# Output and down projection of a two-layer hybrid backbone: 512-column blocks with the k loop outside

## The chip, the cores and the metric

The kernel runs on one core of a Trainium2 chip, in one launch, all in float32 (the large products in the float32r format). The metric is the device time in microseconds (us); the figure for the kernel before is the median of three runs.

## The reference, cut to what matters

640 tokens (128 context tokens and 512 latent tokens) pass through two layers. Each layer has a token mixer and a feed-forward part. Only the two products marked below are touched by the change.

```python
def layer(x, cond, s0_h, s0_r, pos, p):
    ...
    h = rmsnorm(x, p["norm_mix"]) * (1.0 + sc_m) + sh_m
    y, S_a, S_b = token_mixers(h, p, s0_h, s0_r, pos)   # ends in concat([o_a, o_b]) @ p["w_out"]   <- touched
    x = x + g_m * y
    h = rmsnorm(x, p["norm_ffn"]) * (1.0 + sc_f) + sh_f
    gate, up = jnp.split(h @ p["w_up"], 2, axis=-1)
    x = x + g_f * ((jax.nn.silu(gate) * up) @ p["w_down"])   # <- touched
```

`w_out` is 1024 x 1024 and `w_down` is 2816 x 1024, one of each per layer. After the last layer comes a final RMSNorm and the output of `x`.

## The kernel before, in words

The tokens are five tiles of 128 (`NT` = 5, index t), the model width 1024 is eight blocks of 128 (`KT` = 8), the feed-forward width 2816 is 22 blocks, taken in two chunks of 11 (`CH`). Every float32 product is made of three float32r matmuls: each operand is split into a high and a low part, and high·high, high·low and low·high are accumulated (the three `mm` lines of every matmul helper).

Weights come in slots of at most 1024 columns per partition. `Stream.load` issues the DMA of a slot into one of three `raw` buffers on SyncE's queue; `Stream.cut` makes the high part with ScalarE (`wh`, L75) and the low part with VectorE (`wl`, L76) into one of four buffers (`W_BUFS`). `take(n)` hands out the next n cut slots, and `done(n)` gives them back and pumps: it cuts and loads the next slots as far as buffers allow.

Two helpers do nearly all products. `ws` keeps the weights as the stationary operand and moves 320 token columns (256 and 384 where `mid` is set). `as_` keeps 128 tokens as the stationary operand and moves 256 weight columns: for each token tile it goes through all k blocks into one PSUM tile, calls `evac`, and goes to the next token tile. PSUM is a pool of four tiles of 1024 columns (`psp`, two banks each); everything in the kernel takes its PSUM from there.

The output projection `w_out` does four blocks of 256 columns. Blocks 0 and 1 go through `as_`. Blocks 2 and 3 go through `as2`, in the order of pairs (block, tile) that is written out by hand in `OUT_ORDER`, with the four slots of both blocks held. The down projection (in `ffn`) does four blocks of 256 columns for each of the two chunks of 11 k blocks, with three slots (4 + 4 + 3 k blocks) held for each block. `evac` calls `x_add`: VectorE multiplies the PSUM columns by the gate (L957) and adds them to `x` (L959), and ScalarE squares the new columns with a row sum (`sq`, L548). After the last columns of a token tile, `add_norm` forms the reciprocal root, scales the tile, and puts its transposes and modulation (`norm_b`, `norm_c`) into a list that is worked off later by a clock of the generators' own cost units (`LAG`). The next product, the `ws` of three units with `mid` set, begins with token tiles 0 and 1 and needs the others in its second half. After the last layer `final` takes the place of `add_norm`.

Beside the main stream run "lanes": the `ada` lane computes modulation vectors, two VectorE operations per 256 KB of `ada_w` (L504), stepped by the cost units that the main generators yield (`Q_ADA`). Its eight column chunks in the feed-forward part of layer 0 each end in eight transposes into a PSUM tile `pc` and a reduction (L517). At the start of the last block of layer 0 the rest of that lane is drained. The buffers of `ada_w` are the same two `ad` buffers that `x_add` uses.

The order on each engine comes from the framework: it takes the program order as priority and places an instruction when its model holds it ready and has a buffer for it. It also sets all semaphores and buffer releases. Only the start (`boot`) is in an order written by hand.

Of the kernel before, what the change touches and what calls it, by code (L numbers as in the profile page):

```python
# [14 lines left out]
ALU = mybir.AluOpType  # L15
AX = mybir.AxisListType

P = 128
DM = 1024
KT = DM // P  # L20
NT = 5
TOK = NT * P
HALF = TOK // 2
DEPTH = 2
# [18 lines left out]
KD = 2  # L43
FAST = (0, 1, 3)
CUT = 256
OUT_ORDER = [(2, 0), (3, 0), (2, 1), (3, 1), (2, 2), (2, 3), (2, 4), (3, 2), (3, 3), (3, 4)]
Q_SCAN = 2.65
Q_ADA = (3.0, 2.0, 4.0)
ADP_BUFS = 2
# [6 lines left out]
class Stream:  # L56
    def __init__(self, net, slots):
        self.net, self.slots = net, slots
        self.loaded = self.split = self.used = 0
        self.raw, self.ready = {}, {}  # L60
# [42 lines left out]
class Net:  # L103
# [848 lines left out]

    def x_add(self, gates, n0, t, ps, slot):
        nc = self.nc
        g = gates[0 if t == 0 else 1][:, n0:n0 + 256]
        tmp = self.adp.tile([P, 512], F32, tag="ad", name="xa")
        nc.vector.tensor_tensor(tmp[:, :256], ps, g, op=ALU.mult)  # L957
        xs = self.x[:, t, n0:n0 + 256]
        nc.vector.tensor_tensor(xs, xs, tmp[:, :256], op=ALU.add)  # L959
        if slot is not None:  # L960
            self.sq(t, n0, 256, slot, tmp[:, 256:])

    def w_out(self, l):
        self.finish("ada", (l, "gm"))

        def src(i, t):
            return self.oT[i][:, 0, t * P:(t + 1) * P], self.oT[i][:, 1, t * P:(t + 1) * P]
        for n in range(2):
            def evac(g, ps):
                t, = g  # L970
                self.flushT()
                self.x_add(self.g_m, 256 * n, t, ps[:, :256], n)
            yield from self.as_(src, 2, [[t] for t in range(NT)], evac)
        if l == 0:
            self.finish("ada", (0, "cf"))
        self.new_hT()

        def evac2(n, t, ps):
            self.x_add(self.g_m, 256 * n, t, ps[:, :256], n)
            if n == 3:  # L980
                self.add_norm(t, l, 1)
        yield from self.as2(src, OUT_ORDER, evac2)

    def as2(self, ksrc, order, evac):
        slots = self.W.take(4)
        mm = self.nc.tensor.matmul
        for n, t in order:
            ps = self.ps("ga")
            o = ps[:, :256]
            for i in range(KT):  # L990
                hi, lo = slots[2 * (n - 2) + i // 4]
                j = i % 4
                a_hi, a_lo = ksrc(i, t)
                mm(o, a_hi, hi[:, j], start=i == 0, stop=False)  # L994
                mm(o, a_hi, lo[:, j], start=False, stop=False)  # L995
                mm(o, a_lo, hi[:, j], start=False, stop=i == KT - 1)  # L996
                if i == 3:
                    yield 1.31
            if t == NT - 1:
                self.W.done(2, n == 2)  # L1000
            evac(n, t, ps)
            yield 1.31

    def add_norm(self, t, l, m):
        xn = self.ON("xn")
        nc, rs = self.nc, self.rstd(t, 4)
        nc.vector.tensor_scalar(xn[:, :DM], self.x[:, t], rs, None, op0=ALU.mult)
        self.pend.append((self.clock + LAG[m], t, xn, l, m))

# [4 lines left out]
    def ffn(self, l, mid):  # L1014
        nc = self.nc
        self.g_f = []
        self.lanes.append(((l, "gf"), self.ada_gate(l, 1, self.ON, self.g_f)))
        if l + 1 < DEPTH:
            for m in range(2):
                self.lanes.append(((l + 1, "c", m), self.ada_cols(l + 1, m, self.ON)))  # L1020
        for ci, nch in enumerate(CH):
            last = ci == len(CH) - 1
            act = []

            def pair():
                st = {}

                def eg(ps):
                    st["sg"] = self.B("sgf")
                    nc.scalar.activation(st["sg"][:, :TOK].rearrange("p (a b) -> p a b", a=2), ps, AF.Silu)  # L1030

                def eu(ps):
                    sg = st["sg"]
                    at = self.B("act", F32R).rearrange("p (d t) -> p d t", d=2)
                    fv = sg[:, TOK:]
                    nc.vector.tensor_tensor(fv.rearrange("p (a b) -> p a b", a=2),
                                            sg[:, :TOK].rearrange("p (a b) -> p a b", a=2), ps, op=ALU.mult)
                    nc.scalar.copy(at[:, 0], fv)
                    nc.vector.tensor_tensor(at[:, 1], fv, at[:, 0].bitcast(F32), op=ALU.subtract)
                    act.append(at)  # L1040
                return eg, eu
            evs = [e for f in range(nch) for e in pair()]
            if ci == 0:
                yield from self.ws(*evs[:3], mid=mid)
                evs = evs[3:]
            for e in evs:
                yield from self.ws(e)

            def src(i, t):
                return act[i][:, 0, t * P:(t + 1) * P], act[i][:, 1, t * P:(t + 1) * P]  # L1050
            if ci == 0:
                self.finish("ada", (l, "gf"))
            for n in range(4):
                fin = last and n == 3
                if fin and l + 1 < DEPTH:
                    self.drain("ada")
                    self.new_hT()

                def evac(g, ps):
                    t, = g  # L1060
                    self.x_add(self.g_f, 256 * n, t, ps[:, :256], n if last else None)
                    if fin:
                        if l + 1 < DEPTH:
                            self.add_norm(t, l + 1, 0)
                        else:
                            self.final(t)
                yield from self.as_(src, -(-nch // 4), [[t] for t in range(NT)], evac,
                                    not (fin and l + 1 < DEPTH))

    def final(self, t):  # L1070
        nc = self.nc
        if t == 0:
            self.nf = self.ON("nf")
            src = self.a["norm_final"]
            nc.sync.dma_start(out=self.nf[:, :DM], in_=bass.AP(src.tensor, 0, [[0, P], [1, DM]]))
        y = self.B("y")
        rs = self.rstd(t, 4)
        dst = self.a_out(t)
        step = DM if t < NT - 1 else DM // 2
        for c in range(0, DM, step):  # L1080
            sl = slice(c, c + step)
            nc.vector.scalar_tensor_tensor(y[:, sl], self.x[:, t, sl], rs, self.nf[:, sl], op0=ALU.mult, op1=ALU.mult)
            nc.sync.dma_start(out=dst[:, sl], in_=y[:, sl])
# [6 lines left out]
    def slots(self):  # L1090
        a = self.a
        out = []

        def ws(w, c):
            out.append((w[:, c:c + P].rearrange("(k p) n -> p k n", p=P), KT, P))

        def as_(w, r0, nk, c):
            for k in range(0, nk, 4):
                kk = min(4, nk - k)
                r = r0 + k * P  # L1100
                out.append((w[r:r + kk * P, c:c + 256].rearrange("(k p) n -> p k n", p=P), kk, 256))
        for l in range(DEPTH):
            wi, wo, wu, wd = a["w_in"][l], a["w_out"][l], a["w_up"][l], a["w_down"][l]
            for op in ORDER:
                k, j = op[0], int(op[1])
                if k in "ab":
                    as_(wi, 0, KT, OFF["ia" if k == "a" else "vb"] + 256 * j)
                for nm in {"h": ("zf", "zb", "qa"), "r": ("qb", "kb")}.get(k, ()):
                    ws(wi, OFF[nm] + P * j)
            for u in range(4):  # L1110
                as_(wi, 0, KT, OFF["gb" if u // 2 else "ga"] + 256 * (u % 2))
            for n in range(4):
                as_(wo, 0, KT, 256 * n)
            f0 = 0
            for nch in CH:
                for f in range(f0, f0 + nch):
                    ws(wu, f * P)
                    ws(wu, DFF + f * P)
                for n in range(4):
                    as_(wd, f0 * P, nch, 256 * n)  # L1120
                f0 += nch
        return out

# [71 lines left out]
```

## Time and profile before

| what | value |
|---|---|
| median of three runs | 1849.77 us (1849.04 to 1850.96) |
| span of the profiled execution, first to last instruction | 1849.3 us |
| TensorE busy, matmul and weight load | 98% and 97% |
| VectorE, ScalarE, GpSimd busy | 58%, 39%, 3% |
| mean granted TensorE clock | 0.997 |

The profiled execution has no separate device time on record. Its span lies inside the range of the three runs, 0.5 us under their median, so that a change of the span can be read as a change of the median. TensorE's busy share counts matmuls whose durations overlap: how fast it really goes is read from the distance between the starts of two matmuls.

### The profile page before, as it was taken

The page shows a single profiled execution, that of the slowest core. Times are in us where ns is not written, and L with a number is a line of the kernel's source. Part 1 is how long each engine was busy: PE and PEld are TensorE (multiplying, and loading weights), DVE is VectorE, ACT ScalarE, POOL GpSimd, SP SyncE. Part 2 cuts the span into 40 slices and gives each one's busy share as a digit, 9 for nine tenths or more (in the row PEclk, how much of TensorE's full clock was granted, in tenths as well). Part 3 has the DMA queues.
Part 4 walks back from the last instruction along what each step waited for, and adds up shares of the span by engine and source line. Part 5 has one row for each costly group of instructions (what it writes and reads, how often), then busy time and mean ns, then how long its engine had stood idle before and what let it go on. Part 6 is the DMA issues. An engine that isn't in the chain of part 4 may idle for free.

```text
span 1849.3 us, 32230 instructions
## 1 busy us (share of the span) xinstructions
PE 1813.7 (98%) x13627; PEld 1792.1 (97%) x13627; DVE 1076.9 (58%) x1706; ACT 715.4 (39%) x1247; POOL 52.1 (3%) x59
## 2 busy tenths in 40 slices
PE   7999999999999999999999999999999999999998
PEld 4999999999999999999999999999999999999998
DVE  5797968865744466554676655687465523323234
ACT  7676545543422111222246555555342221122221
POOL 2010000000000000000000000000000000000000
PEclk9999999999999999999999999999999999999999
DMA  9233343221533335443322211322233421222212
GB/s 321 83 104 109 97 121 108 84 77 47 169 111 95 96 113 157 125 130 103 115 81 72 63 55 52 122 71 88 76 103 117 123 73 62 83 80 72 74 52 78
DMA packets 221744, 183.20 MB, mean 99 GB/s; under 512 B 7472, under 2 KB 194064, under 8 KB 221600
## 3 DMA queue, kind: packets, MB, share of 16 engines
q1 hardware_dynamic: 216704, 178.62, 31.4%
q10 hardware_dynamic: 4640, 2.43, 0.4%
q8 instruction: 107, 1.75, 0.4%
q0 software_dynamic: 256, 0.09, 0.1%
q14 instruction: 37, 0.30, 0.1%
HBM read 176.39 MB, written 4.72 MB: 98 GB/s over the span
## 4 chain that ended last, share of the span: by engine, by line
PE 81%; DVE 9%; ACT 4%; issue 2%; DMA 2%; POOL 1%; SPq 0%; DVEq 0%; POOLq 0%; ACTq 0%
PE gw L606 14%; PE gw L605 14%; PE gw L607 14%; PE ga L641 9%; PE ga L642 9%; PE ga L640 9%; PE pl L733 2%; DMA adw<-in_ada_w 2%; DVE wl L76 1%; DVE acc L504 1%; ACT wh L75 1%; PE ga L996 1%; PE ga L994 1%; PE ga L995 1%; DVE QQ L737 1%
## 5 line engine op out<-in xcount | busy, mean ns | idle before, releaser
L605 PE MATMUL gw<-hT,wh 128*128 128x320 f32 (+2 forms) x2048 | 637.5, 312 | 0.3 <-DVE QS L692 0.2
L606 PE MATMUL gw<-hT,wh 128*128 128x320 f32 (+2 forms) x2048 | 634.1, 310 | 0.6 <-DVE hT L414 0.3
L607 PE MATMUL gw<-hT,wl 128*128 128x320 f32 (+2 forms) x2048 | 634.0, 310 | 0.0
L75 ACT CAST wh<-raw 128x1024 fp32r<-128x1024 f32 (+1 forms) x224 | 231.5, 1034 | 638.2 <-PE gw L606 289.7
L76 DVE TENSOR_TENSOR wl<-raw,wh 128x1024 fp32r<-128x1024 f32 (+1 forms) x224 | 268.8, 1203 | 222.3 <-ACT wh L75 219.5
L605 PEld LDWEIGHTS gw<-hT,wh 128*128 128x128 f32 x2048 | 385.0, 188 | 2.8 <-ACT hT L413 1.0
L606 PEld LDWEIGHTS gw<-hT,wh 128*128 128x128 f32 x2048 | 385.2, 188 | 1.7 <-DVE hT L414 0.8
L607 PEld LDWEIGHTS gw<-hT,wl 128*128 128x128 f32 x2048 | 385.1, 188 | 0.0
L504 DVE SCALAR_TENSOR_TENSOR acc<-adw,sTt,acc 128x512 f32<-128x512 f32 x280 | 199.5, 747 | 90.3 <-DMA adw<-in_ada_w 90.0
L641 PE MATMUL ga<-wl,act 128*128 128x256 f32 x880 | 249.5, 284 | 0.9 <-DVE wl L76 0.9
L640 PE MATMUL ga<-wh,act 128*128 128x256 f32 x880 | 249.8, 284 | 0.0
L642 PE MATMUL ga<-wh,act 128*128 128x256 f32 x880 | 249.3, 283 | 0.0
L640 PE MATMUL ga<-wh,hT 128*128 128x256 f32 x640 | 186.0, 291 | 0.0
L642 PE MATMUL ga<-wh,hT 128*128 128x256 f32 x640 | 181.3, 283 | 0.0
L641 PE MATMUL ga<-wl,hT 128*128 128x256 f32 x640 | 181.3, 283 | 0.0
L641 PEld LDWEIGHTS ga<-wl,act 128*128 128x128 f32 x880 | 169.0, 192 | 1.3 <-DVE wl L76 1.3
L640 PEld LDWEIGHTS ga<-wh,act 128*128 128x128 f32 x880 | 169.0, 192 | 0.0
L642 PEld LDWEIGHTS ga<-wh,act 128*128 128x128 f32 x880 | 169.0, 192 | 0.0
L640 PEld LDWEIGHTS ga<-wh,hT 128*128 128x128 f32 x640 | 122.6, 192 | 0.2
L641 PEld LDWEIGHTS ga<-wl,hT 128*128 128x128 f32 x640 | 122.6, 192 | 0.3
L642 PEld LDWEIGHTS ga<-wh,hT 128*128 128x128 f32 x640 | 122.4, 191 | 0.0
L957 DVE TENSOR_TENSOR xa<-ga,gate 128x256 f32<-128x256 f32 x120 | 50.4, 422 | 123.4 <-PE ga L642 108.6
(215 smaller groups left out, 2242.2 us busy)
## 6 DMA issues: line engine op xcount, KB each, us to landing
raw<-in_w_up SPq DMA_DIRECT2D x88, 512.0 KB, 4.0
adw<-in_ada_w SPq DMA_DIRECT2D x160, 256.0 KB, 3.1
raw<-in_w_in SPq DMA_DIRECT2D x72, 512.0 KB, 3.9
raw<-in_w_down SPq DMA_DIRECT2D x32, 512.0 KB, 3.4
adw<-in_ada_w SPq DMA_DIRECT2D x16, 512.0 KB, 7.6
raw<-in_w_out SPq DMA_DIRECT2D x16, 512.0 KB, 3.5
raw<-in_w_down SPq DMA_DIRECT2D x16, 384.0 KB, 3.7
gate<-in_ada_b SPq DMA_DIRECT2D x8, 512.0 KB, 4.4
```

What stands on the lines that cost most here:

```text
L75: nc.scalar.copy(hi[:, :n], raw[:, :n])
L76: nc.vector.tensor_tensor(lo[:, :n], raw[:, :n], hi[:, :n].bitcast(F32), op=ALU.subtract)
L504: nc.vector.scalar_tensor_tensor(d, w, s, d, op0=ALU.mult, op1=ALU.add)
L605: mm(o, hi[:, k], h_hi, start=k == 0, stop=False)
L606: mm(o, hi[:, k], h_lo, start=False, stop=False)
L607: mm(o, lo[:, k], h_hi, start=False, stop=k == KT - 1)
L640: mm(o, a_hi, hi[:, j], start=i == 0, stop=False)
L641: mm(o, a_hi, lo[:, j], start=False, stop=False)
L642: mm(o, a_lo, hi[:, j], start=False, stop=i == nk - 1)
L733: nc.tensor.matmul(pl[:, i * P:(i + 1) * P], X[:, TOK + i * P:TOK + (i + 1) * P], X[:, i * P:(i + 1) * P], start=True, stop=True)
L737: V.tensor_tensor(qv, qv, view(F, b, [[2 * b, tb], [TOK - b, 2], [0, b]]), op=ALU.mult)
L957: nc.vector.tensor_tensor(tmp[:, :256], ps, g, op=ALU.mult)
```

## The change

Both products go through a new helper, `cols_512`. It moves 512 weight columns instead of 256, one whole bank, and a slot holds two k blocks of 512 columns instead of four of 256 (with 11 k blocks the first slot holds one). There are two blocks of columns in place of four. The k loop is outside: for each slot, all five token tiles get their share, each in its own bank (tiles 0 and 1 share one PSUM tile, 2 and 3 another, 4 has a third), and the five banks are evacuated when the last slot is through. Where `held` is 4, which is in the last block of `w_out` and in the last block of each layer's down projection, the last four slots (eight k blocks) are held together, and each token tile goes through all eight of them and is evacuated before the next tile. `x_add` and `sq` work on 512 columns, and the sum of squares has two parts instead of four. `as2` and `OUT_ORDER` go. Each slot is given back and pumped by itself.

```diff
-OUT_ORDER = [(2, 0), (3, 0), (2, 1), (3, 1), (2, 2), (2, 3), (2, 4), (3, 2), (3, 3), (3, 4)]
...
     def x_add(self, gates, n0, t, ps, slot):
...
-        nc.vector.tensor_tensor(tmp[:, :256], ps, g, op=ALU.mult)
-        xs = self.x[:, t, n0:n0 + 256]
-        nc.vector.tensor_tensor(xs, xs, tmp[:, :256], op=ALU.add)
+        nc.vector.tensor_tensor(tmp, ps, g, op=ALU.mult)
+        xs = self.x[:, t, n0:n0 + 512]
+        nc.vector.tensor_tensor(xs, xs, tmp, op=ALU.add)
         if slot is not None:
-            self.sq(t, n0, 256, slot, tmp[:, 256:])
+            self.sq(t, n0, 512, slot, tmp)
...
-        for n in range(2):
-            def evac(g, ps):
-                t, = g
-                self.flushT()
-                self.x_add(self.g_m, 256 * n, t, ps[:, :256], n)
-            yield from self.as_(src, 2, [[t] for t in range(NT)], evac)
+        def evac(t, ps):
+            self.x_add(self.g_m, 0, t, ps, 0)
+        yield from self.cols_512(src, KT, 0, evac, self.flushT)
...
-        yield from self.as2(src, OUT_ORDER, evac2)
+        yield from self.cols_512(src, KT, 4, evac2)
...
+    def cols_512(self, ksrc, nk, held, evac, early=None):
         mm = self.nc.tensor.matmul
+        sizes = [nk % 2] * (nk % 2) + [2] * (nk // 2)
+        pss = [None] * 3
+
+        def part(t, k0, slot):
+            hi, lo = slot
+            if pss[t // 2] is None:
+                pss[t // 2] = self.ps("ga")
+            o = pss[t // 2][:, t % 2 * 512:t % 2 * 512 + 512]
+            for j in range(hi.shape[1]):
+                i = k0 + j
                 a_hi, a_lo = ksrc(i, t)
                 mm(o, a_hi, hi[:, j], start=i == 0, stop=False)
                 mm(o, a_hi, lo[:, j], start=False, stop=False)
+                mm(o, a_lo, hi[:, j], start=False, stop=i == nk - 1)
+            return o, 0.68 * hi.shape[1]
+        k = 0
+        for kk in sizes[:len(sizes) - held]:
+            slot, = self.W.take(1)
+            outs = []
+            for t in range(NT):
+                o, cost = part(t, k, slot)
+                outs.append(o)
+                if t == NT - 1:
+                    self.W.done()
+                    k += kk
+                if k == nk:
+                    for u in range(NT):
+                        evac(u, outs[u])
+                if early and t == 1:
+                    early()
+                    early = None
+                yield cost
+        if not held:
+            return
+        slots = self.W.take(held)
+        for t in range(NT):
+            for i, slot in enumerate(slots):
+                o, cost = part(t, k + 2 * i, slot)
+                if t == NT - 1:
+                    self.W.done()
+                if i == held - 1:
+                    evac(t, o)
+                yield cost
...
-            for n in range(4):
-                fin = last and n == 3
+            for n in range(2):
+                fin = last and n == 1
...
-                yield from self.as_(src, -(-nch // 4), [[t] for t in range(NT)], evac,
-                                    not (fin and l + 1 < DEPTH))
+                yield from self.cols_512(src, nch, 4 if fin else 0, evac)
```

## Rows read from the trace of the kernel before

**Rows 1.** The page: busy time of each engine; granted clock in 40 slices.
```profile
PE 1813.7 (98%) x13627; PEld 1792.1 (97%) x13627; DVE 1076.9 (58%) x1706; ACT 715.4 (39%) x1247; POOL 52.1 (3%) x59
...
PEclk9999999999999999999999999999999999999999
```

**Rows 2.** Windows: output projection, down projection (two), an up projection, the end.
```profile
core 0: us, PE busy (x) PEld busy (x) DVE busy (x) ACT busy (x) POOL busy (x), PEclk, DMA share, GB/s
...
871.62:955.11 83.49, 83.49 (x702) 83.49 (x701) 53.23 (x94) 27.13 (x63) 1.85 (x4) 1.00 0.30 92
1307.29:1368.66 61.37, 60.81 (x509) 60.51 (x508) 34.97 (x69) 24.19 (x63) 1.67 (x3) 1.00 0.24 70
1528.48:1607.67 79.19, 79.19 (x662) 79.19 (x661) 29.85 (x51) 12.47 (x13) 0.00 (x0) 1.00 0.21 64
1607.67:1762.56 154.89, 154.89 (x1059) 154.89 (x1057) 44.06 (x45) 36.82 (x44) 0.00 (x0) 1.00 0.27 81
...
1841.75:1849.30 7.55, 0.16 (x2) 0.00 (x0) 2.70 (x7) 0.51 (x2) 0.55 (x1) 0.77 0.35 139
```

**Rows 3.** What TensorE waited for, layer 1's output projection and after: total, times, longest.
```profile
PE pt L567 <- DVE xn L1007: 0.8, 2, 0.6
PE pt L567 <- ACT hT L585: 0.7, 1, 0.7
```

**Rows 4.** What TensorE waited for in layer 0's down projection, first chunk.
```profile
PE ga L641 <- DVE wl L76: 0.9, 2, 0.6
```

**Rows 5.** What TensorE waited for, layer 0's second chunk into layer 1.
```profile
PE pt L567 <- DVE xn L1007: 1.4, 1, 1.4
PE gw L606 <- DVE hT L586: 0.2, 1, 0.2
```

**Rows 6.** Groups by line and form: one of three lines each of `as_` and `as2`.
```profile
L640 PE MATMUL ga<-wh,act 128*128 128x256 f32 x880 | 249.8, 284 | 0.0
...
L994 PE MATMUL ga<-wh,oT 128*128 128x256 f32 x160 | 45.8, 286 | 0.0
L640 PE MATMUL ga<-wh,oT 128*128 128x256 f32 x160 | 45.6, 285 | 0.0
```

**Rows 7.** Timeline of TensorE: trains of 512-column matmuls at the start (start, duration).
```profile
30.11 0.39 PE L354 MATMUL pr<-ahi,sr 128*128 128x512 f32 x1
...
31.02 0.39 PE L354 MATMUL pr<-ahi,sr 128*128 128x512 f32 x1
...
49.02 0.40 PE L354 MATMUL pr<-alo,sr 128*128 128x512 f32 x1
...
50.64 0.34 PE L605 MATMUL gw<-hT,wh 128*128 128x384 f32 x1
```

**Rows 8.** Groups by line and form: VectorE and ScalarE at 256 and 512 columns, cuts.
```profile
L76 DVE TENSOR_TENSOR wl<-raw,wh 128x1024 fp32r<-128x1024 f32 x208 | 253.8, 1222 | 207.6 <-ACT wh L75 204.9
...
L75 ACT CAST wh<-raw 128x1024 fp32r<-128x1024 f32 x208 | 218.2, 1049 | 613.0 <-PE gw L606 269.6 <-issue 186.9 <-PE ga L642 149.0
...
L959 DVE TENSOR_TENSOR x<-x,xa 128x256 f32<-128x256 f32 x120 | 50.6, 423 | 3.2
...
L957 DVE TENSOR_TENSOR xa<-ga,gate 128x256 f32<-128x256 f32 x120 | 50.4, 422 | 123.4 <-PE ga L642 108.6 <-PE ga L996 13.2 <-ACT xa L548 0.6
...
L548 ACT ACTIVATE xa<-x 128x256 f32<-128x256 f32 x80 | 33.4, 417 | 162.9 <-DVE x L959 161.6 <-issue 1.3
...
L517 DVE TENSOR_REDUCE modc<-pc 128x8 f32<-128x1024 f32 x12 | 14.7, 1221 | 15.3 <-PE pc L516 15.3
...
L543 DVE TENSOR_TENSOR gate<-gate,pg 128x512 f32<-128x512 f32 x16 | 10.9, 681 | 9.3 <-PE pg L541 9.2
...
L942 ACT ACTIVATE sg<-ga 128x512 f32<-128x512 f32 x16 | 9.6, 597 | 28.2 <-PE ga L642 27.7 <-PE pto L927 0.5
```

**Rows 9.** Timeline of VectorE, end of a down-projection block (start, duration).
```profile
1547.08 2.19 DVE L76 TENSOR_TENSOR wl<-raw,wh 128x1024 fp32r<-128x1024 f32 x2 [1.68 <-ACT wh L75]
1549.19 0.42 DVE L957 TENSOR_TENSOR xa<-ga,gate 128x256 f32<-128x256 f32 x1
1549.60 1.23 DVE L76 TENSOR_TENSOR wl<-raw,wh 128x1024 fp32r<-128x1024 f32 x1
```

**Rows 10.** The page's DMA issues: size, and median time to landing.
```profile
raw<-in_w_down SPq DMA_DIRECT2D x32, 512.0 KB, 3.4
```

More of the change, by code (lines that the diff above doesn't have):

```diff
@@ L954, in x_add @@
         nc = self.nc
-        g = gates[0 if t == 0 else 1][:, n0:n0 + 256]
+        g = gates[0 if t == 0 else 1][:, n0:n0 + 512]
         tmp = self.adp.tile([P, 512], F32, tag="ad", name="xa")
-        nc.vector.tensor_tensor(tmp[:, :256], ps, g, op=ALU.mult)
-        xs = self.x[:, t, n0:n0 + 256]
-        nc.vector.tensor_tensor(xs, xs, tmp[:, :256], op=ALU.add)
+        nc.vector.tensor_tensor(tmp, ps, g, op=ALU.mult)
+        xs = self.x[:, t, n0:n0 + 512]
+        nc.vector.tensor_tensor(xs, xs, tmp, op=ALU.add)
         if slot is not None:
-            self.sq(t, n0, 256, slot, tmp[:, 256:])
+            self.sq(t, n0, 512, slot, tmp)
     def w_out(self, l):
@@ L976, in w_out, with evac2 @@
         self.new_hT()
[L978 to L981, printed above, removed]
-        yield from self.as2(src, OUT_ORDER, evac2)
-    def as2(self, ksrc, order, evac):
-        slots = self.W.take(4)
-        mm = self.nc.tensor.matmul
[L987 to L992, printed above, removed]
+        def evac2(t, ps):
+            self.x_add(self.g_m, 512, t, ps, 1)
+            self.add_norm(t, l, 1)
+        yield from self.cols_512(src, KT, 4, evac2)
+    def cols_512(self, ksrc, nk, held, evac, early=None):
+        mm = self.nc.tensor.matmul
+        sizes = [nk % 2] * (nk % 2) + [2] * (nk // 2)
[7 more added lines that the diff above has]
+                i = k0 + j
                 a_hi, a_lo = ksrc(i, t)
@@ L995, in as2 @@
                 mm(o, a_hi, lo[:, j], start=False, stop=False)
[L996 to L1002, printed above, removed]
+                mm(o, a_lo, hi[:, j], start=False, stop=i == nk - 1)
[28 more added lines that the diff above has]
+                yield cost
     def add_norm(self, t, l, m):
         xn = self.ON("xn")
-        nc, rs = self.nc, self.rstd(t, 4)
+        nc, rs = self.nc, self.rstd(t, 2)
         nc.vector.tensor_scalar(xn[:, :DM], self.x[:, t], rs, None, op0=ALU.mult)
@@ L1057, in ffn, with evac @@
                     self.new_hT()
-                def evac(g, ps):
-                    t, = g
-                    self.x_add(self.g_f, 256 * n, t, ps[:, :256], n if last else None)
+                def evac(t, ps):
+                    self.x_add(self.g_f, 512 * n, t, ps, n if last else None)
                     if fin:
@@ L1076, in final @@
         y = self.B("y")
-        rs = self.rstd(t, 4)
+        rs = self.rstd(t, 2)
         dst = self.a_out(t)
@@ L1101, in as_, with c512 @@
                 out.append((w[r:r + kk * P, c:c + 256].rearrange("(k p) n -> p k n", p=P), kk, 256))
+        def c512(w, r0, nk, c):
+            k = 0
+            while k < nk:
+                kk = 2 - (nk - k) % 2
+                r = r0 + k * P
+                out.append((w[r:r + kk * P, c:c + 512].rearrange("(k p) n -> p k n", p=P), kk, 512))
+                k += kk
         for l in range(DEPTH):
@@ L1111, in slots @@
                 as_(wi, 0, KT, OFF["gb" if u // 2 else "ga"] + 256 * (u % 2))
-            for n in range(4):
-                as_(wo, 0, KT, 256 * n)
+            for n in range(2):
+                c512(wo, 0, KT, 512 * n)
             f0 = 0
@@ L1118, in slots @@
                     ws(wu, DFF + f * P)
-                for n in range(4):
-                    as_(wd, f0 * P, nch, 256 * n)
+                for n in range(2):
+                    c512(wd, f0 * P, nch, 512 * n)
                 f0 += nch
```

## Prediction

> **What bounds the kernel now.** I read the page first. TensorE is busy 98% of the span, matmuls and weight loads alike, and its clock is at the full 2.4 GHz level in every slice; VectorE and ScalarE have 42% and 61% of the span to spare [rows 1]. So the next views were those of TensorE: what it waits for, and how far apart its matmuls start. The waits are small: 1.5 us around each of the two output projections [rows 3], 0.9 us in layer 0's first down-projection chunk [rows 4] and 1.6 us at the change from layer 0 to layer 1 [rows 5], 5.5 us in all where the change works (3.0 + 0.9 + 1.6). What is left is pace. A down-projection chunk in layer 1 has 11 k blocks x 3 matmuls x 5 token tiles x 4 column blocks = 660 matmuls of 256 columns in 79.19 us, which is 0.1200 us from start to start. The up projection after it has 22 units x 48 = 1056 matmuls of 320 columns in 154.89 us, 0.1467 us each [rows 2]. The step is 0.0267 us for 64 columns, 0.417 ns a column, which is one column per cycle at 2.4 GHz. Then 256 columns take 0.1067 us, and 0.0133 us of each matmul are paid whatever its width. That fixed part is what bounds here beyond the columns themselves.
>
> **The matmuls.** The change halves the number of matmuls in both products and doubles their width; the columns stay the same. Their number now is 3 x (880 + 160 + 160) = 3600 [rows 6] (the other two lines of each helper have the same counts), so 1800 matmuls of 512 columns remain and 1800 fixed parts go. The price of a 512-column matmul is bounded from three rows. The line through 256 and 320 columns gives 0.1467 + 192 x 0.000417 = 0.2267 us. A train at the start with float32r operands runs from 30.11 to 31.02 us in four steps, 0.2275 us each; a second one from 49.02 to 50.64 us in seven steps, 0.2314 us each [rows 7]. Two matmuls of 256 columns cost 0.2400 us. So a pair saves 0.0086 to 0.0133 us. I take 0.229 us, between the two trains, since in the new stream high and low slots alternate as they do there: 0.011 us x 1800 = 19.8 us saved (15.5 to 23.9).
>
> The Trainium skill (TensorE: Matmul & The Clock Gate, Back-to-back issue gap) has for a single warm stream one cycle per column and a fixed 2.5 ns a matmul. By that rule the merge would save only 1800 x 0.0025 = 4.5 us, and the sum below would end at 1845.7 us. The trace does not agree: the rule gives 109 ns for 256 columns, and this kernel's rows have 120.0 ns.
>
> **Evacuation.** Per token tile and 512 columns, VectorE now makes two pairs of 0.42 us operations and will make one pair of about 0.68 us (a 512-column PSUM read: 0.681 us), so it saves about 0.3 us 60 times; ScalarE's squares go from 0.417 to about 0.6 us, once instead of twice [rows 8]. Neither engine is on the path, so this is worth nothing in mid-stream. It costs at the very end: after the last matmul the tail, now 7.55 us [rows 2], contains one multiply, one add and one square for token tile 4, and these grow by 0.26 + 0.26 + 0.18 = 0.7 us. I count +0.7 us.
>
> **Weight supply.** A slot is still 1024 columns per partition, so DMA and cut prices stay: 3.4 us to landing [rows 10], 1.05 us on ScalarE and 1.22 us on VectorE [rows 8]. A slot now feeds 2 x 3 x 5 = 30 matmuls, 6.9 us. Before, three of four slots came back at once and the next block's cuts bunched up (three in a row in rows 9); that is the 0.9 us of [rows 4]. Now one slot comes back at a time with three ahead, some 20 us. I count -0.9 us. The held blocks need four slots together, but tile 0 reaches the fourth only 3 x 1.37 = 4.1 us in, and the last cut takes 2.3 us: cost 0, bounded by about 2 us for each of four held blocks, if VectorE is late by that much.
>
> **PSUM, the new wait.** For some 27 us (eight k blocks) to 38 us (eleven) three of the four PSUM tiles are open, and at a block's end five banks come back together. VectorE needs 5 x 1.36 = 6.8 us for that. TensorE can start the next block in the fourth tile at once. Token tile 2 then needs the tile of 0 and 1. With 11 k blocks the first slot has one k block, so tiles 0 and 1 last 2 x 3 x 0.229 = 1.4 us. Lower bound: zero. In the last slot the five tiles finish 1.37 us apart, tile 0 already 5.5 us before the block ends, and one evacuation takes 1.36 us, so VectorE keeps step if it may begin at once. The code issues all five after the last matmul and after the next cut, but the framework orders by readiness: [rows 9] show an evacuation slipped between two cuts that precede it in the program. Upper bound: VectorE does cut and evacuations in program order, 1.05 + 1.22 + 0.68 + 0.68 + 0.68 = 4.3 us until tile 0/1 is free, less 1.4 us = 2.9 us. It applies where an 11-block k loop is followed by another, twice per layer, four times. Elsewhere cover is long: the held block of the output projection stays 11 us in the fourth tile, a `ws` unit 7 us. I take 0.4 us x 4 = +1.6 us (0 to 11.8), near the lower end because of the order in [rows 9].
>
> **The norms.** Token tiles now finish 24 x 0.229 = 5.5 us apart in the last block. In the output projection tiles 2 to 4 had finished 2.9 us apart, which is where the 1.5 us of [rows 3] come from: transposes waiting for a norm still on VectorE or ScalarE. Tile 4's chain grows by 0.7 us, and the cuts of the next phase, no longer put off at the end of these blocks, can put 1 to 2 us of VectorE ahead of it. The first half of the next `ws` covers it: three units x 24 matmuls x 0.12 = 8.6 us. I count -1.0 us, with bounds -4.6 (all waits of rows 3 and 5 gone) and +6 (2 us more at each of three changes). The generators' cost units fall by 3.8 per chunk, which leaves the ada lane a few steps more to drain before layer 0's last block; that block's first evacuation comes 15.9 us after its start, which covers them: 0.
>
> **Sum.** -19.8 + 0.7 - 0.9 + 1.6 - 1.0 = -19.4 us against the span of 1849.3 us; the median of the runs is 0.5 us above the span, so 1849.8 - 19.4 = 1830.4 us.
>
> **Rivals.**
>
> *The block ends wait in full.* VectorE takes the five banks in program order: 4 x 2.9 = 11.6 us in place of 1.6, so 1840.4 us. For it: the cut and all five evacuations are issued after the last matmul. Against it: [rows 9]. The Trainium skill (PSUM — Partial Sum Buffer, Summary) speaks on this side: it asks for prompt evacuation because PSUM is small. No run here shows yet what late evacuation costs. Chance 0.13.
>
> *The fixed part is not fixed.* What exceeds one cycle per column grows with the columns, 512 columns cost 0.240 us, and nothing is saved: the sum is +0.4 us, 1850 us, within 0.2%. For it: 0.2314 us in the second train is above the line already. Against it: 256 and 320 columns have excesses of 13.3 and 13.4 ns, and neither train reaches 0.232. Chance 0.08. The rule of the Trainium skill's matmul page above is the milder form of this case: its 1845.7 us share that chance, and the same 120.0 ns speak against it.
>
> *Slower: no spare tile.* If the fourth tile is taken at block ends (by `pc`, a transpose or a norm), TensorE stands the whole 4.3 us at all eight block ends: 34.4 us against 19.8 saved, so 1864 us; it decides from 19.8/8 = 2.5 us per end. For it: four tiles serve everything. Against it: in layer 1 no lane runs in the down projection, and in layer 0 a `pc` tile lives for some 2 us (reduction 1.22 us [rows 8]) eight times in the whole feed-forward part. Chance 0.06.
>
> **How the numbers follow.** About 0.2% (3.7 us) is what a measurement of this kernel can tell from no change. The forecast with its own range, 1825 to 1836 us, has 0.73, and the four cases make 1. Faster takes the forecast and the first rival, less 0.01 for a mix of waits: 0.85; same 0.08; slower 0.07. The range of 8 in 10 starts at 1825 us (the cheapest matmul, with the rest as counted, gives 1849.8 - 23.5 = 1826.3 us, and some of the waits of before may go as well) and reaches to 1841 us to take in the first rival.
>
> **What would show it.** In the profile after: about 11,800 matmuls; 512-column matmuls 0.227 to 0.231 us apart; a layer-1 chunk of 330 matmuls in 75 to 77 us instead of 79.2; VectorE's multiply of token tile 0 starting some 5 us before a block's last matmul; no wait of `ga` for `wl`. The forecast is wrong if 512-column matmuls start 0.235 us apart or more, if TensorE waits for `xa` at block ends by over 1 us each, or if the first `ws` after a held block waits more than 2 us for `hT`.

## The result, and the profile after

The changed kernel takes 1865.12 us (median of 4 runs, 1863.68 to 1867.31) against 1850.15 us for the kernel before: a ratio of 1.0078, 95% interval 1.0066 to 1.009. It is 15 us slower. The forecast was 1830.4 us. (The figure of 1849.77 us for the kernel before, which the forecast starts from, is the median of the first three of these runs.)

First the page of the changed kernel: busy time of each engine, and the granted clock in 40 slices.

```profile
PE 1798.8 (97%) x11827; PEld 1700.8 (91%) x11827; DVE 1058.9 (57%) x1586; ACT 705.4 (38%) x1167; POOL 53.8 (3%) x59
...
PEclk9999999999999999999899999999999999999999
```

There are 1800 matmuls fewer, as meant, and TensorE still looks busy. One slice in the middle has a lower clock, which the page of before [rows 1] did not have. The stretches that answer to [rows 2] show where the time is. Windows of the changed kernel, columns as in [rows 2]:

```profile
core 0: us, PE busy (x) PEld busy (x) DVE busy (x) ACT busy (x) POOL busy (x), PEclk, DMA share, GB/s
...
906.87:922.01 15.14, 0.17 (x1) 0.03 (x1) 11.04 (x17) 3.23 (x9) 0.00 (x0) 0.66 0.41 122
922.01:926.00 3.99, 3.99 (x15) 3.57 (x16) 1.99 (x4) 0.00 (x0) 0.00 (x0) 0.60 0.00 0
868.55:972.10 103.55, 83.48 (x381) 68.58 (x379) 54.53 (x81) 27.52 (x50) 3.47 (x4) 0.92 0.25 77
...
1323.54:1389.57 66.03, 59.73 (x277) 48.07 (x275) 36.84 (x58) 25.17 (x50) 2.21 (x4) 1.00 0.22 67
1548.67:1623.49 74.82, 74.82 (x332) 61.94 (x331) 25.59 (x30) 12.93 (x13) 0.00 (x0) 1.00 0.28 81
...
1853.62:1861.90 8.28, 0.16 (x1) 0.00 (x0) 3.31 (x7) 0.72 (x2) 0.55 (x1) 0.71 0.32 127
```

The first down-projection chunk of layer 1 takes 74.82 us instead of 79.19 [rows 2]: the wide matmuls bring what they should. Layer 1's output projection takes 66.03 us instead of 61.37, and layer 0's second down-projection chunk 103.55 us instead of 83.49; these stretches end where the next product's first matmul starts, and of the changed kernel they hold one group of eight transposes (0.9 to 1.6 us) more. In that chunk lies a hole of 15.14 us in which TensorE does nothing. What it waited for in the whole run (total, times, longest):

```profile
PE pc L515 <- DVE acc L503: 15.0, 1, 15.0
PE pt L566 <- DVE xn L1028: 14.5, 11, 4.3
...
PE ga L992 <- DVE xa L956: 3.3, 4, 0.9
```

Three kinds of wait are new or have grown. `pc`, the transposes at the end of an ada-lane chunk, waited once for 15.0 us. `pt`, the transposes of a normed token tile, waited 14.5 us; around the changed blocks that was 4.4 us before (1.5 us at each output projection, layer 0's like layer 1's [rows 3], and 1.4 us at the change of layers [rows 5]). And matmuls of the projection itself waited for the evacuation `xa`, which none did before. The waits for `wl` [rows 4] are gone.

The hole in detail. TensorE's timeline (start, duration, idle before and what ended it):

```profile
906.65 0.39 PE L994 MATMUL ga<-wh,act 128*128 128x512 f32 x1
922.01 1.94 PE L515 MATMUL pc<-ident,acc 128*128 128x128 f32 x8 [14.97 <-DVE acc L503]
923.60 0.78 PE L992 MATMUL ga<-wh,act 128*128 128x512 f32 x1
924.17 0.63 PE L993 MATMUL ga<-wl,act 128*128 128x512 f32 x1
```

At 906.65 us the last matmul of the block before last starts. Next in TensorE's order are not the matmuls of the last block, whose operands are ready, but the lane's eight transposes, and those need the lane's last chunk. The queue that loads for the lane (SyncE, DMA issues):

```profile
896.61 0.34 SPq L496 DMA_DIRECT2D adw<-in_ada_w  x1
...
909.78 0.34 SPq L496 DMA_DIRECT2D adw<-in_ada_w  x1
...
912.23 6.45 SPq L496 DMA_DIRECT2D adw<-in_ada_w  x4
```

And VectorE at the same time:

```profile
903.75 1.28 DVE L956 TENSOR_TENSOR xa<-ga,gate 128x512 f32<-128x512 f32 x2
904.94 1.28 DVE L958 TENSOR_TENSOR x<-x,xa 128x512 f32<-128x512 f32 x2
...
912.57 1.42 DVE L503 SCALAR_TENSOR_TENSOR acc<-adw,sTt,acc 128x512 f32<-128x512 f32 x2 [1.19 <-DMA adw<-in_ada_w]
...
921.11 1.41 DVE L503 SCALAR_TENSOR_TENSOR acc<-adw,sTt,acc 128x512 f32<-128x512 f32 x2 [0.34 <-DMA adw<-in_ada_w]
```

Five loads of the lane are still to come when the block ends. The first is issued at 909.78 us and the other four from 912.23 us, when the squares of the `x_add`s have returned the `ad` buffers that both share; then the five go through two buffers, some 2.1 us each, until 922.5 us. From 906.87 us, 2.9 us go by before the first load is issued, and 12.2 us with the loads. Over the next 4 us, with the transposes and the first matmuls behind the hole, the mean granted clock is 0.60, most of it at the lower level of 1.2 GHz (0.50), and the first two 512-column matmuls start 0.57 us apart.

VectorE's and ScalarE's prices at 512 columns, which the forecast had at about 0.68 and 0.6 us (groups by line and form):

```profile
L956 DVE TENSOR_TENSOR xa<-ga,gate 128x512 f32<-128x512 f32 x60 | 39.9, 686 | 27.2 <-PE ga L994 27.1 <-ACT xa L547 0.2
L958 DVE TENSOR_TENSOR x<-x,xa 128x512 f32<-128x512 f32 x60 | 39.9, 686 | 0.6
...
L547 ACT ACTIVATE xa<-x 128x512 f32<-128x512 f32 x40 | 25.2, 631 | 58.8 <-DVE x L958 58.8
```

### The profile page after: what moved, and what is told of

The parts are those of the page before. It is cut to its first block, busy times and chain, and to the rows that moved or that the text cites. A ratio compares the mean times of both kernels' runs of the same rounds, so it can differ in the third digit from the quotient of the medians.

```text
span 1861.9 us, 28365 instructions
## 1 busy us (share of the span) xinstructions
PE 1798.8 (97%) x11827; PEld 1700.8 (91%) x11827; DVE 1058.9 (57%) x1586; ACT 705.4 (38%) x1167; POOL 53.8 (3%) x59
## 4 chain that ended last, share of the span: by engine, by line
PE 83%; DVE 8%; ACT 4%; issue 2%; DMA 2%; POOL 1%; SPq 0%; DVEq 0%; POOLq 0%; ACTq 0%
PE gw L605 15%; PE gw L604 15%; PE gw L606 15%; PE ga L992 6%; PE ga L994 6%; PE ga L993 6%; PE ga L641 3%; PE ga L640 3%; PE ga L639 3%; PE pl L732 3%; PE pt L566 1%; DVE acc L503 1%; DMA adw<-in_ada_w 1%; DVE wl L75 1%; ACT wh L74 1%
## 5 line engine op out<-in xcount | busy, mean ns | idle before, releaser
L992 PE MATMUL ga<-wh,act 128*128 128x512 f32 x440 | 172.1, 392 | 0.0
L993 PE MATMUL ga<-wl,act 128*128 128x512 f32 x440 | 171.6, 390 | 0.0
L994 PE MATMUL ga<-wh,act 128*128 128x512 f32 x440 | 171.6, 390 | 0.0
L1057 DVE TENSOR_TENSOR sgf<-sgf,gw 128x640 f32<-128x640 f32 x44 | 36.0, 819 | 130.0 <-PE gw L606 130.0
L992 PEld LDWEIGHTS ga<-wh,act 128*128 128x128 f32 x440 | 82.9, 188 | 17.8 <-DVE xa L956 0.9
L994 PEld LDWEIGHTS ga<-wh,act 128*128 128x128 f32 x440 | 82.8, 188 | 17.4
L993 PEld LDWEIGHTS ga<-wl,act 128*128 128x128 f32 x440 | 82.9, 188 | 16.8
```

What stands on the lines that cost most here:

```text
L994: mm(o, a_lo, hi[:, j], start=False, stop=i == nk - 1)
```

## The experiments

Each run is compared with runs of the kernel before on the same chip, whose medians lay between 1849.62 and 1849.89 us. The first three take the three kinds of wait one by one, the fourth takes them together.

**Run 1: the lane a little faster.**

```diff
-Q_ADA = (3.0, 2.0, 4.0)
+Q_ADA = (3.0, 2.0, 3.6)
```

> The changed kernel with the ada lane stepped every 3.6 cost units in the feed-forward part instead of 4.0, so that no lane step is left to drain before layer 0's last block. Theory (late lane): the 15.0 us wait of the pc transposes for acc is gone, and with it some 1.5 us at half clock behind it; 1865 - 16.5 = 1848 to 1850 us. Rival (five banks at once): the burst of x_adds at that block end holds both ad buffers and VectorE, and TensorE stands there anyway; a wait of over 8 us stays and the time falls by at most 7 us, to 1858 us or more.

Measured: 1849.04 us, ratio 0.9995 (0.9986 to 1.0004). That is 16.1 us less than the changed kernel, and no wait for `acc` is left. The second wait is untouched (`pt` for `xn` in the whole run):

```profile
PE pt L566 <- DVE xn L1028: 14.5, 11, 4.3
```

The theory of the late lane holds. In the trace the chunk with the hole falls from 103.55 to 85.9 us, and no other product, and no stretch between two of them, changes by more than about 1 us. The five-bank burst in front of the last block does not keep TensorE waiting by itself.

**Run 2: the next phase's weight cuts put off.**

```diff
-        yield from self.cols_512(src, KT, 4, evac2)
+        yield from self.cols_512(src, KT, 4, evac2, later=True)
...
-                    self.W.done()
+                    self.W.done(1, i == 0 or not later)
...
-                yield from self.cols_512(src, nch, 4 if fin else 0, evac)
+                yield from self.cols_512(src, nch, 4 if fin else 0, evac, later=fin and l + 1 < DEPTH)
```

> The changed kernel with the next phase's weight cuts put off in the held blocks that a mid ws follows: only the first returned slot is pumped, the rest waits for the pump inside ws. Theory (cuts ahead of the norms): the waits of pt for xn after the held blocks (3.7, 4.4 and 3.7 us) fall under 1.5 us each and the half clock behind them goes; 12 us less, 1851 to 1855 us. Rival (longer chain): the norm chain of the last token tiles is late because it works on 512 columns, cuts or not; at most 3 us less, 1862 us or more.

Measured: 1865.13 us, ratio 1.0083 (1.007 to 1.0097): nothing. The edit did not do what was meant. VectorE's timeline behind layer 0's output projection, with the weight cuts (`wl`) and the scaling of a normed token tile (`xn`), first of the changed kernel:

```profile
466.22 1.23 DVE L75 TENSOR_TENSOR wl<-raw,wh 128x1024 fp32r<-128x1024 f32 x1
...
468.57 1.22 DVE L75 TENSOR_TENSOR wl<-raw,wh 128x1024 fp32r<-128x1024 f32 x1
...
469.77 1.22 DVE L75 TENSOR_TENSOR wl<-raw,wh 128x1024 fp32r<-128x1024 f32 x1
...
471.78 0.75 DVE L1028 TENSOR_SCALAR xn<-x,rs 128x1024 f32<-128x1024 f32 x1
```

Then of this run, which is 1.33 us later here:

```profile
467.55 1.23 DVE L75 TENSOR_TENSOR wl<-raw,wh 128x1024 fp32r<-128x1024 f32 x1
...
469.90 1.22 DVE L75 TENSOR_TENSOR wl<-raw,wh 128x1024 fp32r<-128x1024 f32 x1
...
471.76 1.21 DVE L75 TENSOR_TENSOR wl<-raw,wh 128x1024 fp32r<-128x1024 f32 x1
473.41 0.75 DVE L1028 TENSOR_SCALAR xn<-x,rs 128x1024 f32<-128x1024 f32 x1 [0.44 <-POOL rs L560]
```

The first two cuts are in the same place and the third is 0.7 us later; all three still lie ahead of `xn`. In this run, then, the framework takes a cut soon after its buffers are free, also when the program asks for it later. So the run does not show what the cuts cost the norms; it shows that moving the pump in the program hardly moves them.

**Run 3: neighbouring token tiles in different PSUM tiles.**

```diff
-            if pss[t // 2] is None:
-                pss[t // 2] = self.ps("ga")
-            o = pss[t // 2][:, t % 2 * 512:t % 2 * 512 + 512]
+            if pss[t % 3] is None:
+                pss[t % 3] = self.ps("ga")
+            o = pss[t % 3][:, t // 3 * 512:t // 3 * 512 + 512]
```

> The changed kernel with neighbouring token tiles in different PSUM tiles (tiles 0 and 3, 1 and 4, 2) instead of the same one. Theory (dependences by PSUM tile): the two waits of 1.0 us per output projection, where token tile 1 starts while tile 0 is evacuated, and 3 the same, go; 3 to 5 us less, 1860 to 1862 us. Rival (VectorE late, dependences by bank): waits stay, no change.

Measured: 1856.75 us, ratio 1.0041 (1.0026 to 1.0056), 8.4 us less than the changed kernel and more than expected. All waits of `ga` for `xa` are gone. The longest `pt` wait around layer 0's output projection falls from 3.5 to 1.8 us, although the total only falls from 4.7 to 3.9 us (first the changed kernel, then this run):

```profile
PE pt L566 <- DVE xn L1028: 4.7, 4, 3.5
```

```profile
PE pt L566 <- DVE xn L1028: 3.9, 5, 1.8
```

So the framework's dependences go by PSUM tile, not by bank. In the changed kernel token tile 1 could not start (from 440.25 us, the last matmul of tile 0, to 441.49 us) until tile 0 had been read out of the other bank. TensorE, then VectorE:

```profile
440.25 0.39 PE L994 MATMUL ga<-wh,oT 128*128 128x512 f32 x1
441.49 0.50 PE L992 MATMUL ga<-wh,oT 128*128 128x512 f32 x1 [0.85 <-DVE xa L956]
```

```profile
440.74 0.69 DVE L956 TENSOR_TENSOR xa<-ga,gate 128x512 f32<-128x512 f32 x1 [1.84 <-PE ga L994]
```

The lane's wait grew to 17.5 us in this run, which hides 2.5 us of the gain. With the shorter stands the clock stays up as well: over the 14 us around each of the three changes from a held block to a `ws`, the granted clock is 1.00 in this run, where the changed kernel falls to its lower level (last section).

**Run 4: all three.**

> The three edits together. Theory (the three waits are separate and explain the loss): 16.5 + 12 + 4 us less than the changed kernel, 1832 to 1836 us, about 16 us faster than the kernel before. Rival (waits move): a part returns elsewhere, 1840 us or more.

Measured: 1836.77 us, ratio 0.9929 (0.9917 to 0.9942), 13 us faster than the kernel before. It misses the expected 1832 to 1836 us by under 1 us, and comes this close by chance: of the three gains that were added up, the 12 us of the put-off cuts had not come in run 2, and the PSUM tiles are worth more than the 4 us that were put down for them. Of the waits, `pt` for `xn` stays:

```profile
PE pt L566 <- DVE xn L1028: 10.8, 14, 1.7
```

**Run 5: only the lane late, in the kernel before.** This is the test of the lane without any wide block.

```diff
-Q_ADA = (3.0, 2.0, 4.0)
+Q_ADA = (3.0, 2.0, 4.3)
```

> The kernel before, in 256-column blocks, with only the ada lane stepped every 4.3 cost units instead of 4.0 in the feed-forward part, so that some five steps are left to drain before layer 0's last block, as in the changed kernel. Theory (late lane alone): the pc transposes stand in TensorE's order ahead of the last block and wait for five loads through two buffers, 9 to 13 us, with half clock behind: 1860 to 1865 us. Rival (it takes the five-bank burst as well): without the burst in front the loads run under the block before, and the wait stays below 4 us: under 1854 us.

Measured: 1873.77 us, ratio 1.0129 (1.0115 to 1.0143), 24 us slower, more than either side expected. The wait is the same one, and longer: six loads were left, not five, and the first of them is issued 4 us into the hole, behind three weight loads in SyncE's queue. TensorE's wait, SyncE's issues, and the window of the hole:

```profile
PE pc L516 <- DVE acc L504: 20.4, 1, 20.4
```

```profile
936.07 13.34 SPq L497 DMA_DIRECT2D adw<-in_ada_w  x6
```

```profile
931.00:952.90 21.90, 1.50 (x14) 1.33 (x13) 13.24 (x19) 2.42 (x5) 0.00 (x0) 0.62 0.47 144
```

No five banks come back in front of these loads. The wait needs nothing but lane steps left over at the drain.

**Run 6: lane and PSUM tiles, without the put-off of the cuts** (the edits of runs 1 and 3).

> The changed kernel with the lane stepped every 3.6 units and neighbouring token tiles in different PSUM tiles, the weight cuts not put off. Theory (the cuts are worth nothing by themselves, as run alone): the same as with all three edits, 1836 to 1838 us. Rival (the cuts matter once the PSUM tiles are apart): 1865.1 - 16.1 - 8.4 = 1840.6 us or more.

Measured: 1838.15 us, ratio 0.9935 (0.9923 to 0.9948), at the upper end of the expected 1836 to 1838 us. Its interval and that of run 4 overlap for the most part: the put-off is worth nothing that can be measured, and two of the three edits carry run 4. Their single gains, with the 2.5 us that the lane's longer wait hid in run 3, give 16.1 + 8.4 + 2.5 = 27.0 us, and this run is 27.0 us below the changed kernel.

**Runs 7 and 8: the transposes of a normed tile later in the program** (on top of run 4).

```diff
-LAG = (5.3, 4.0)
+LAG = (6.8, 5.5)      # run 8: (8.3, 7.0)
```

> All three edits, and the transposes of a normed tile come 1.5 cost units later in the program (6.8 and 5.5 instead of 5.3 and 4.0). Theory (the norm chain on 512 columns is longer than the delay that it was given): the waits of pt for xn, 10.8 us in all and some 4.5 us per held block, fall by more than half: 1829 to 1832 us. Rival (VectorE is simply late, or the framework's order does not follow the program here): no change beyond 2 us.

> The same with 3 cost units more (8.3 and 7.0). Theory: the waits of pt for xn during the held blocks are gone; the last tile's transposes are forced by the second half of ws as before, so at most 1 to 2 us beyond the run before it, or a loss if the first ws then waits for hT. Rival: no change.

Measured: 1838.92 us, ratio 0.994 (0.9927 to 0.9954), and 1835.5 us, ratio 0.9922 (0.9909 to 0.9934). Neither differs from run 4 by more than the intervals allow, and run 7 lies well above its 1829 to 1832 us. The waits of `pt` inside the blocks nearly go, but `gw` now waits for `hT` in the first `ws` after the three held blocks that a `ws` follows, where it had waited for nothing of that kind. Run 8:

```profile
PE gw L604 <- ACT hT L584: 7.8, 3, 2.9
```

The theory failed as put: the delay does not end the stand but moves most of it, from 10.8 us of `pt` to 7.8 us of `gw`. That suggests that work is missing to put in front of the last tile's norm, which the next two runs try.

**Runs 9 and 10: more such work.** The first half of the `ws` behind a held block takes three token tiles; in run 10 the delay of run 8 is added.

```diff
-        cut = CUT if mid or order else HALF
+        cut = 384 if mid else CUT if order else HALF
```

> All three edits, and the first half of the ws behind a held block works on token tiles 0 to 2 (384 columns) instead of 0 and 1 (256). Token tiles now finish 5.5 us apart, so tile 2 is ready in time, and three units then cover 12.5 us instead of 8.6 us of the last tile's norm chain. Theory (the rest of the missing gain is the last tile's chain behind a cover that is too short): the waits of 0.9 and 1.9 us at each of three places go, 5 to 8 us less, 1829 to 1832 us. Rival (PSUM tiles or VectorE hold the chain): 1835 us or more.

> The same with the transposes 3 cost units later (8.3 and 7.0). Theory: the 0.5 to 0.7 us waits of pt inside the held blocks go as well, and the longer cover takes up the delay: 2 to 4 us less than the run before it, 1826 to 1829 us, which is the forecast's matmul saving nearly whole. Rival: the delay comes back as waits for hT in ws, as it did without the longer cover; no gain over the run before it.

Measured: run 9 1842.49 us, ratio 0.9959 (0.9946 to 0.9971), which is 5.7 us slower than run 4; run 10 1830.6 us, ratio 0.9895 (0.9882 to 0.9909). Run 9 refutes its theory as put. Its transposes still come at the old place in TensorE's order, before the longer first half is through, and in it they stand longer, up to 3.4 us at a time; behind both output projections the mean granted clock then falls to 0.88 and 0.79 over the next 15 us, where it is 1.00 in run 4:

```profile
PE pt L566 <- DVE xn L1028: 12.6, 14, 3.4
```

Only with the place moved as well is the cover used: run 10 is 4.9 us below run 8, which has the place alone. It is 11.9 us below run 9, where 2 to 4 were expected, and still 1.6 us above the expected 1826 to 1829 us. In run 10 no `pt` wait for `xn` of these norms is left, but as its rival said, a part comes back where the `ws` wait three times:

```profile
PE gw L604 <- ACT hT L584: 5.3, 3, 2.7
```

**Run 11: two held slots instead of four** (on top of run 4).

```diff
-        yield from self.cols_512(src, KT, 4, evac2, later=True)
+        yield from self.cols_512(src, KT, 2, evac2, later=True)
...
-                yield from self.cols_512(src, nch, 4 if fin else 0, evac, later=fin and l + 1 < DEPTH)
+                yield from self.cols_512(src, nch, 2 if fin else 0, evac, later=fin and l + 1 < DEPTH)
```

> All three edits with two held slots (four k blocks) instead of four in the last blocks, so that token tiles finish 2.7 us apart instead of 5.5. Theory (the spacing of the token tiles sets how much of the norms lies under the block): the waits behind the held blocks grow by some 3 to 6 us at each of three places; 10 to 18 us slower than with four, 1847 to 1855 us. Rival (only the last tile's chain counts, and that starts at the same point): no change beyond 3 us.

Measured: 1843.49 us, ratio 0.9964 (0.995 to 0.9978), 6.7 us slower than run 4, between the two expectations. The waits for `xn` do not grow in all (10.8 us in run 4); they are fewer and longer:

```profile
PE pt L566 <- DVE xn L1028: 10.6, 7, 3.1
```

The edit also acts on the last block of the kernel, which no `ws` follows. In the traces each output projection with the up projection behind it takes 1.0 us more than in run 4, the change of layers some 2 us more, and the end, from the last matmul on, 11.1 us instead of 8.5. So the spacing of the token tiles is worth 1 to 2 us at each of the three places of the theory, not 3 to 6, and 2.6 us at a fourth that the theory left out.

**Run 12: run 10 without the put-off of the cuts.**

> The fastest version so far without its put-off of the weight cuts: lane stepped every 3.6 units, neighbouring token tiles in different PSUM tiles, transposes 3 cost units later, first half of the next ws 384 columns wide. Theory (the put-off moves no cut on VectorE and is worth nothing): 1829 to 1832 us, as with it. Rival (with the norms later in the order the cuts do get in their way): 1834 us or more.

Measured: 1831.97 us, ratio 0.9901 (0.9884 to 0.9917), as the theory expected. The put-off does nothing that can be measured here either. The version that beats both kernels is the wide blocks with four small edits: the lane at 3.6, the PSUM tiles apart, `LAG` at (8.3, 7.0), and the first half at 384.

## Why the prediction was wrong, point by point

**The matmuls: right, the size at the edge of its range.** A chunk of 330 matmuls in 74.82 us is 0.2267 us each, the value of the line through 256 and 320 columns; 0.229 was taken. With 0.1200 us before, 1800 x 0.0133 = 23.9 us are saved, the upper end of the forecast's 15.5 to 23.9 and 4.1 us more than the 19.8 that were counted. The Trainium skill's rule of a fixed 2.5 ns a matmul (TensorE: Matmul & The Clock Gate, Back-to-back issue gap), which that section gives for an isolated matmul, would have made it 4.5 us; the measurement decides against it for this stream, in which every matmul has its own weight load.

**The ada lane: the step that failed.** The forecast says: "The generators' cost units fall by 3.8 per chunk, which leaves the ada lane a few steps more to drain before layer 0's last block; that block's first evacuation comes 15.9 us after its start, which covers them: 0." Both halves are wrong, and the term was put at nothing. The drain stands before the last column block. That was after three of four blocks and is now after one of two. Up to there the two chunks yielded 78.6 + 3/4 x 78.6 = 137.6 units and now yield 74.8 + 37.4 = 112.2. So 25.4 units are missing, some six steps of 4.0, where two chunks at 3.8 make two. And the cover was looked for on the wrong engine. The steps end in transposes, which stand on TensorE in front of the whole block, so that nothing of the block can cover them. (The Trainium skill says, in TensorE: Matmul & The Clock Gate, Part 2, that matmuls stay in program order; the trace agrees, since the 165 matmuls behind the eight transposes waited 15 us.) Price: 16.1 us (run 1), more than the whole loss of 15.0. That such lateness is enough without any wide block is shown by run 5, where six loads left over cost the kernel before 24 us. None of the forecast's three signs of being wrong came: the wait that decided was not on its list.

**PSUM: right at the block ends, missed inside the held blocks.** Where the forecast feared up to 11.8 us (its 4 x 2.9 is 11.6) and took 1.6, there is nothing: the chunks of layer 1 run without a wait. But it assumed that token tile 0 can be evacuated while tile 1 is being written, since each has its own bank. The timelines of the changed kernel at such a block end in layer 1, TensorE and VectorE, say otherwise:

```profile
1581.79 0.39 PE L994 MATMUL ga<-wh,act 128*128 128x512 f32 x1
```

```profile
1580.58 1.22 DVE L75 TENSOR_TENSOR wl<-raw,wh 128x1024 fp32r<-128x1024 f32 x1 [5.58 <-ACT wh L74]
1582.21 1.29 DVE L956 TENSOR_TENSOR xa<-ga,gate 128x512 f32<-128x512 f32 x2 [0.41 <-PE ga L994]
```

VectorE is free from 1581.80 us and token tile 0 was ready a tile earlier, but it waits until 1582.21 us for tile 1's last matmul, which starts at 1581.79 us, and then reads both. (In run 3, where tile 0 shares with tile 3, VectorE's first multiply at the same block end waits until 1.1 us before the end of the block.) In the held blocks the same pairing stopped TensorE four times for 0.9 us or a little less, and delayed the norms. Price: 8.4 us (run 3), and 10.9 with the 2.5 us that the lane's wait hid. Of that 3.3 us are the waits of `ga` for `xa` and 3.1 the shorter waits of `pt` for `xn` (14.5 to 11.4 us); the clock that stays up behind the held blocks, some 6 us by estimate (last section), would cover the rest, but no run took it alone.

**The norms: the direction was wrong.** Counted were -1.0 us (-4.6 to +6). The waits of `pt` rose from 4.4 to 14.5 us. With lane and PSUM tiles mended they still were 10.8 us (run 4), so that an output projection with the up projection behind it takes 222.0 and 221.1 us from its first matmul to the first of the down projection, as in the kernel before (222.0 and 221.2): the waits take back what the wider matmuls save there. A cover of 12.5 us together with a later place makes the kernel 6.2 us faster (run 10 against run 4). The forecast looked at the last token tile, which the first half of the next `ws` covers. In the changed kernel the long stands are those of the tile before it, whose transposes stand in TensorE's order ahead of that `ws`: behind layer 0's output projection the held block's last matmul starts at 468.79 us and these transposes at 472.68 us. On VectorE three weight cuts of 1.2 us lie ahead of its `xn` (run 2's lines); how much of the stand is theirs stays open.

**Evacuation and tail, weight supply: right.** The tail went from 7.55 to 8.28 us (+0.7 forecast), and the waits for `wl` of [rows 4] are gone.

**The rivals.** None of them was the cause. The slower rival (no spare PSUM tile) had the sign, and with 1864 us nearly the number, by luck: TensorE waits for no PSUM tile at the block ends that it counts. That run 10 measures the forecast's 1830.4 us is in part luck as well. Its matmuls save 4.1 us more than was counted, and its norms still cost 6.4 us of waits for `hT` where the forecast left 3.6. It does show that nearly the whole saving is there for a kernel in which the lane, the PSUM pairing and the norms are adapted to the new blocks.

What stays open: the price of the weight cuts that lie ahead of the norms on VectorE, which run 2 could not move; and a remainder. The matmuls (-23.9), tail and weight supply (-0.2), lane (+16.1), PSUM pairing (+10.9) and the waits of the norms that are left in run 4 (10.8 - 4.4 = +6.4) make 9.3 us of the 15.0 measured, and the other 5.7 us are not traced.

## What to carry to other kernels

When loops are re-cut, look up every place where side work is forced to finish (a drain, a `finish`), recompute how much of it is then still undone, and price it on the engine whose in-order queue it ends up in, not on the engine that does it. Here the distance of matmul starts at two widths gave the pace at a third: 0.2267 us by the line and measured. Two accumulators that are written and read at different times should not share an allocation of the framework, even when each has its own bank. And an edit whose parts all seem to work is worth taking apart: two of run 4's three edits carry it, and the third adds nothing that can be measured.

## What the runs showed of the hardware that was not expected

The clock after a stand costs time that no wait shows. Behind the 15.1 us hole the mean granted clock is 0.60 over the next 4 us; in run 5 it is 0.62 over the 21.9 us with the hole and 0.53 over the 4.1 us behind them. Of the 16.1 us that run 1 gains, 15.0 are the wait; the rest would fit the slow transposes and matmuls behind it, which no run took alone. The same happens, less visibly, behind the held blocks. Windows of the changed kernel behind layer 0's output projection, the change of layers and layer 1's output projection, where TensorE had stood 3.5, 4.3 and 3.5 us (columns as in [rows 2]):

```profile
472.68:474.27 1.59, 1.59 (x9) 1.59 (x9) 1.59 (x2) 0.00 (x0) 0.00 (x0) 0.50 0.70 165
474.27:479.00 4.73, 4.73 (x27) 4.73 (x26) 2.78 (x6) 3.24 (x8) 0.58 (x1) 0.60 0.97 293
970.50:976.00 5.50, 5.50 (x26) 5.50 (x27) 4.17 (x8) 3.15 (x8) 0.00 (x0) 0.50 0.90 270
1388.70:1394.00 5.30, 5.30 (x33) 5.30 (x34) 4.06 (x8) 3.24 (x8) 0.28 (x1) 0.68 0.95 288
```

At the lower level (0.50, 1.2 GHz) matmuls of 256 columns start 0.213 us apart instead of 0.120. Behind the three stands 53 of them take 11.6 us instead of 6.4, and two groups of eight transposes 1.6 us each instead of 0.9: some 6 us in all, an estimate from these starts. In run 3, where the stands in these places are at most 1.9 us, the clock stays at 1.00, and so it does in run 4.

The weight loads, which were busy as long as the matmuls at 256 columns (79.19 of 79.19 us [rows 2]), are busy 61.94 of 74.82 us at 512, so that TensorE's loading has room now. The pace is 0.2267 us where one column per cycle at 2.4 GHz would be 0.2133: the fixed 0.0133 us of a matmul is the same as at 256 and 320 columns and is still paid. What it consists of, no run shows.
